# Five joined edits in a two-layer trunk: convolution taps, the end of the last FFN by token tiles, meta values and meta rows, and other parts and slots

## The chip, the cores and the metric
The kernel runs on one core of one Trainium2 chip. TensorE (PE) multiplies matrices into banks of PSUM, VectorE (DVE), ScalarE (ACT) and GpSimd (POOL) do the arithmetic on tiles in SBUF, and SyncE (SP) starts most of the transfers. The metric is the device time of one execution in microseconds (us), the median of three runs.

## The reference, cut to what matters
512 tokens of width 1024 get 16 learned "meta" rows in front, an input LayerNorm, and two layers of three residual steps each. All values are float32.

```
h = layer_norm(concat(meta, x))
for l in range(2):
    h = LN(ALPHA*h + 0.5*swiglu_ffn(h, w13_1, w2_1))      # d_ff 2752
    z = h @ w_in                                          # -> xp, ca, cg, q, k, v, g
    y_pool = trailing means of xp over 2, 4, 8, 16 tokens, minus xp, then a small matmul
    y_conv = silu(LN(causal depthwise conv, 31 taps, of ca*sigmoid(cg))) @ w_pw
    y_ret  = silu(g) * groupnorm(chunk-causal retention of q, k, v; 4 heads of 128, rotary q and k)
    h = LN(ALPHA*h + concat(y_pool, y_conv, y_ret) @ w_out)
    h = LN(ALPHA*h + 0.5*swiglu_ffn(h, w13_2, w2_2))
return h[16:]
```

## The kernel before, in words
Tokens are kept feature-major, [128 features, tokens], in eight feature tiles and two halves of 264 tokens (256 real ones and 8 meta rows each). A float32 product is made of three matmuls on split operands: high part by high part, and the two mixed ones with the rest (lines 133 to 135). So every weight tile is loaded by SP, copied rounded to its high part on ACT (L91), and its rest is taken on DVE, or on POOL for three units at the start (L94).

`enter` and `turn` bring the tokens in: the input LayerNorm runs row by row, then TensorE transposes (L257) and ACT, DVE and POOL make the split tiles (L259 to L268). Each FFN goes through its 21 full units of 128 hidden columns and a short one (21) in five `PARTS`: it makes the hidden tiles of a part, then adds that part's share to all eight output tiles (`y`), and the last part is followed by the LayerNorm of each half (`center`, `norm_apply`), whose result the next stage reads. Stages are named by layer: f0a, m0 (the mixer), f0b, f1a, m1, f1b.

The mixer makes the projections u (for the convolution) and xp (for the pools), then the values v in five token tiles (`m0v`, lines 680 to 682; the fifth is the 16 meta rows, gathered in `xm`), then per head the projections of k and q with a rotary turn (`rotary`, L703 to L705), the gate, the scores (`m0sc`, L719), and the values weighted with them. The short tile `km` holds the 16 meta columns of a head's rotated k; POOL copies them (L794), and the first score matmul of a head reads it. The convolution is 62 instructions on DVE (31 taps for two channel tiles; the first pair is a TENSOR_SCALAR on L608, the rest are on L610), issued a few at a time in the loop over the heads by `PACE`. POOL makes the sums over the pools' windows (`m0sm`, L639 and L642). `last_ffn` of layer 1 is token-major, so that its output leaves as rows; at its end come `measure`, `root`, `scale` and `leave` for each of four tiles of 128 tokens.

The program is recorded in the order of the code, and a list scheduler then sets a fixed order for each engine from its own estimates of time. Each engine works through its list in that order and waits at any instruction whose inputs, or whose buffer, are not ready. Buffers come from pools with a fixed number of slots for each tag. Those that matter here: PSUM's `acc` has four banks, used in turn by the v tiles and by the projections of k and q; `wide` has 16 slots, which hold u, xp, the convolution's sums `m0y`, and the pools' window sums.

Of the kernel before, what the change touches and what calls it, by code (L numbers as in the profile page):

```python
# [16 lines left out]
P = 128  # L17
# [23 lines left out]
PACE = (4, 3, 3, 2, 0)  # L41
# [14 lines left out]
PARTS = ([0, 1, 21, 2, 3], *(list(range(u, u + 4)) for u in (4, 8, 12)), list(range(16, 21)))  # L56


def trunk(ctx, tc, a):
# [165 lines left out]
    def enter(s):  # L225
# [47 lines left out]
    def center(tiles, n, width, name):  # L273
# [292 lines left out]
    def mixer(l, name):  # L566
# [131 lines left out]

        def rotary(ps, s, n, nm):
# [5 lines left out]
            nc.vector.tensor_tensor(out=r[:, :n], in0=r[:, :n], in1=r2[:, :n], op=ALU.add)  # L705
# [59 lines left out]
        def gate(hd, s, gg, w):  # L765
            (ps,) = project([w], s, no[s], f"{name}gp{hd}{s}")
            g = t(f"{name}gs{hd}{s}", "g")
            nc.scalar.activation(g[:, : no[s]], ps[:, : no[s]], AF.Silu)
# [77 lines left out]
    def last_ffn(l, name):  # L846
# [18 lines left out]
        for part, units in enumerate(PARTS):  # L865
# [5 lines left out]
            nk = len(full)  # L871
            for ch in range(2):
# [24 lines left out]
                if part == len(PARTS) - 1 and ch == 1:  # L897

                    for tt in range(3):
                        for i in steps:  # L900
                            step(i, tt)
                        for j in range(2):
                            add(tt, j, ps[tt][:, j * 256 : (j + 1) * 256])
                    for j in range(2):
                        o = ps[3] if j == 0 else acc(f"{name}o{ch}4")
                        for i in steps:
                            step(i, 3, j * 256, 256, o[:, :256])
                        add(3, j, o[:, :256])
                else:
                    for i in steps:  # L910
                        for tt in range(4):
                            step(i, tt)
                    for tt in range(4):
                        for j in range(2):
                            add(tt, j, ps[tt][:, j * 256 : (j + 1) * 256])
# [18 lines left out]
        def scale(tt):  # L934
            for j, y in enumerate(yt[tt]):
                if tt == 1:
# [3 lines left out]
        def leave(tt):  # L940
            g_, b_ = gb
            if tt == 1:
                nb = sq_pool.tile([P, 3], F32, tag="nb", name=f"{name}nb", bufs=2)[:, :1]
                nc.vector.scalar_tensor_tensor(out=nb, in0=mvs[tt][:, 0:1], scalar=-1.0, in1=rss[tt], op0=ALU.mult, op1=ALU.mult)
            for j in range(4):
                y = yt[tt][j][:, :256]
                if tt == 1:
                    nc.scalar.activation(y, y, AF.Identity, scale=rss[tt], bias=nb)  # L948
                    nc.gpsimd.tensor_tensor(out=y, in0=y, in1=g_[j][:, :256], op=ALU.mult)  # L949
                    nc.gpsimd.tensor_tensor(out=y, in0=y, in1=b_[j][:, :256], op=ALU.add)  # L950
                elif (tt, j) in ((2, 1), (2, 3), (3, 3)):
# [122 lines left out]
```

## Time and profile before

| | us |
|---|---|
| median of three runs | 1964.85 (1963.27 to 1964.92) |
| the profiled execution, its own time | 1963.63 |
| its span, first to last instruction | 1961.8 |
| PE busy in the span | 1907.0 (97%) |
| DVE, ACT, POOL busy | 1526.4, 909.2, 217.4 |

TensorE's granted clock has a mean of 0.994 over the span. PE is idle for 1961.8 - 1907.0 = 54.8 us. A timeline row is: start in us, duration in us, engine, line, operation, output <- inputs, shapes, count; in brackets stands how long the engine had been idle before, and what ended that.

### The profile page before, as it was taken

Reading aid. Unit: us, or ns where it says so; the run is one execution under the profiler, and the core shown is the slowest. Engines: PE = TensorE matmul, PEld = TensorE weight load, DVE = VectorE, ACT = ScalarE, POOL = GpSimd, SP = SyncE. Lnnn points to the kernel's source line nnn. Section 1 sums busy time; section 2 is a strip of 40 time slices with the busy share of each in tenths; the row PEclk is TensorE's granted clock in tenths of the full one; section 3 lists DMA queues with packets and bytes.
Section 4 is the critical chain, followed back from the end, with each engine's and each line's share of the span. In section 5 each row is a group of like instructions: output and inputs, shape, how many; then the busy total and the mean of one; then the engine's idle time right before and its main releaser. Section 6 shows DMA issues by size and latency. Waiting matters only on the chain.

```text
span 1961.8 us, 36780 instructions
## 1 busy us (share of the span) xinstructions
PE 1907.0 (97%) x14471; PEld 1824.0 (93%) x14471; DVE 1526.4 (78%) x3426; ACT 909.2 (46%) x1817; POOL 217.4 (11%) x283
## 2 busy tenths in 40 slices
PE   7999999999999999999999999999999999999996
PEld 6999999897899999999999999998889999999995
DVE  7788778689767887778696788787897686877787
ACT  5454446444333644455464454454343265544461
POOL 4000000442003000000120000005320130000001
PEclk9999999999999999999999999999999999999998
DMA  4422323322112223223223323332231213323321
GB/s 144 130 89 95 119 87 105 101 76 86 63 33 76 65 97 119 87 97 105 90 71 103 108 81 103 98 129 65 65 105 55 65 44 119 119 76 108 108 97 43
DMA packets 61068, 177.98 MB, mean 91 GB/s; under 512 B 6976, under 2 KB 10944, under 8 KB 60896
## 3 DMA queue, kind: packets, MB, share of 16 engines
q1 hardware_dynamic: 59744, 174.59, 27.9%
q8 instruction: 113, 1.85, 0.4%
q10 hardware_dynamic: 1152, 1.05, 0.2%
q14 instruction: 59, 0.48, 0.1%
HBM read 173.52 MB, written 2.10 MB: 90 GB/s over the span
## 4 chain that ended last, share of the span: by engine, by line
PE 82%; DVE 11%; issue 2%; ACT 2%; POOL 2%; DMA 0%; SPq 0%; DVEq 0%; POOLq 0%; ACTq 0%
PE f1bo L890 2%; PE f1bo L888 2%; PE f1bo L889 2%; PE f1a_y L134 2%; PE f0a_y L134 2%; PE f0b_y L134 2%; PE f1a_y L135 2%; PE f0b_y L133 2%; PE f0b_y L135 2%; PE f1a_y L133 2%; PE f0a_y L133 2%; PE f0a_y L135 2%; DVE m1y L610 1%; PE m1sc L719 1%; PE m0o L738 1%
## 5 line engine op out<-in xcount | busy, mean ns | idle before, releaser
L610 DVE SCALAR_TENSOR_TENSOR m1y<-m1u,vec,m1y 128x528 f32<-128x528 f32 x60 | 46.1, 803 | 0.0
L91 ACT CAST f0b_o_h<-f0b_o_r 128x512 fp32r<-128x512 f32 (+1 forms) x37 | 23.4, 636 | 48.7 <-PE f0b_y L134 29.6
L91 ACT CAST f0a_o_h<-f0a_o_r 128x512 fp32r<-128x512 f32 (+1 forms) x37 | 23.4, 635 | 48.6 <-PE f0a_y L134 29.5
L610 DVE SCALAR_TENSOR_TENSOR m0y<-m0u,vec,m0y 128x528 f32<-128x528 f32 x60 | 45.9, 801 | 0.0
L91 ACT CAST f1a_o_h<-f1a_o_r 128x512 fp32r<-128x512 f32 (+1 forms) x37 | 23.4, 636 | 48.4 <-PE f1a_y L134 29.6
L335 DVE TENSOR_TENSOR x<-x,f0a_y 128x264 f32<-128x264 f32 x64 | 27.2, 426 | 23.2 <-PE f0a_y L135 23.1
L335 DVE TENSOR_TENSOR h<-h,f1a_y 128x264 f32<-128x264 f32 x64 | 27.1, 425 | 23.1 <-PE f1a_y L135 23.0
L335 DVE TENSOR_TENSOR h<-h,f0b_y 128x264 f32<-128x264 f32 x64 | 27.1, 425 | 23.0 <-PE f0b_y L135 22.9
L94 DVE TENSOR_TENSOR f1bw_l<-f1bw_r,f1bw_h 128x512 fp32r<-128x512 f32 x42 | 27.7, 688 | 17.6 <-ACT f1bw_h L91 17.0
L949 POOL TENSOR_TENSOR yt<-yt,g_last 128x256 f32<-128x256 f32 x4 | 3.0, 739 | 333.2 <-ACT yt L948 333.2
L94 DVE TENSOR_TENSOR f0a_o_l<-f0a_o_r,f0a_o_h 128x512 fp32r<-128x512 f32 (+1 forms) x42 | 26.7, 642 | 13.8 <-ACT f0a_o_h L91 11.7
L94 DVE TENSOR_TENSOR f0b_o_l<-f0b_o_r,f0b_o_h 128x512 fp32r<-128x512 f32 (+1 forms) x42 | 26.6, 642 | 13.8 <-ACT f0b_o_h L91 11.7
L94 DVE TENSOR_TENSOR f1a_o_l<-f1a_o_r,f1a_o_h 128x512 fp32r<-128x512 f32 (+1 forms) x42 | 26.7, 642 | 13.7 <-ACT f1a_o_h L91 11.4
L278 POOL TENSOR_TENSOR f0b_ln_s<-h,h 128x264 f32<-128x264 f32 x2 | 1.6, 820 | 310.0 <-DVE h L335 310.0
L587 POOL MEMSET m0u<- 128x30 f32 x2 | 0.2, 123 | 304.0 <-PE f0a_20Q L135 304.0
L587 POOL MEMSET m1u<- 128x30 f32 x2 | 0.2, 123 | 303.1 <-PE f1a_20Q L135 303.1
L894 DVE TENSOR_TENSOR yt<-yt,f1bo 128x256 f32<-128x256 f32 x80 | 27.8, 415 | 5.4 <-PE f1bo L890 5.3
L91 ACT CAST f1bw_h<-f1bw_r 128x1024 fp32r<-128x1024 f32 (+1 forms) x22 | 22.1, 1011 | 21.1 <-PE f1bo L890 4.2
L291 ACT ACTIVATE m_ln_q<-h 128x264 f32<-128x264 f32 (+1 forms) x32 | 11.9, 414 | 39.7 <-DVE h L289 36.2
L257 PE MATMUL tr<-ident,xtok 128*128 128x128 f32 (+1 forms) x48 | 10.9, 328 | 11.9 <-DVE xtok L242 11.3
L257 PEld LDWEIGHTS tr<-ident,xtok 128*128 128x128 f32 (+1 forms) x48 | 6.8, 167 | 16.0 <-issue 14.7
L281 POOL TENSOR_TENSOR m_ln_s<-m_ln_s,h 128x264 f32<-128x264 f32 (+1 forms) x20 | 18.3, 914 | 30.8 <-DVE h L329 24.8
(10715 smaller groups left out, 9301.2 us busy)
## 6 DMA issues: line engine op xcount, KB each, us to landing
f1bw_r<-in_w2last SPq DMA_DIRECT2D x20, 512.0 KB, 3.9
f0a_o_r<-in_w SPq DMA_DIRECT2D x32, 256.0 KB, 2.7
f0b_o_r<-in_w SPq DMA_DIRECT2D x32, 256.0 KB, 2.8
f1a_o_r<-in_w SPq DMA_DIRECT2D x32, 256.0 KB, 2.8
m0wo_r<-in_w_out SPq DMA_DIRECT2D x8, 512.0 KB, 3.5
m1wo_r<-in_w_out SPq DMA_DIRECT2D x8, 512.0 KB, 3.5
m0w_r<-in_w_in SPq DMA_DIRECT2D x6, 512.0 KB, 4.0
m1w_r<-in_w_in SPq DMA_DIRECT2D x6, 512.0 KB, 4.2
```

The lines of the kernel that those rows point to most:

```text
L91: nc.scalar.copy(out=hi[:, :n], in_=w[:, :n])
L94: e.tensor_tensor(out=lo[:, sl], in0=w[:, sl], in1=raw(hi[:, sl]), op=ALU.subtract)
L133: nc.tensor.matmul(out, lhsT=wh, rhs=xh, start=start, stop=False, skip_group_check=onto)
L134: nc.tensor.matmul(out, lhsT=wh, rhs=xl, start=False, stop=False, skip_group_check=onto)
L135: nc.tensor.matmul(out, lhsT=wl, rhs=xh, start=False, stop=stop, skip_group_check=onto)
L335: nc.vector.tensor_tensor(out=y, in0=y, in1=ps, op=ALU.add)
L610: nc.vector.scalar_tensor_tensor(out=ys[c], in0=src, scalar=wk, in1=ys[c], op0=ALU.mult, op1=ALU.add)
L719: nc.tensor.matmul(sc[:kn, :cw], lhsT=kk[ks][:, kc : kc + kn], rhs=qq[s][:, c0 : c0 + cw], start=True, stop=True)
L888: nc.tensor.matmul(o, lhsT=hh, rhs=wh, start=part > 0 and i == 0, stop=False)
L889: nc.tensor.matmul(o, lhsT=hh, rhs=wl, start=False, stop=False)
L890: nc.tensor.matmul(o, lhsT=hl, rhs=wh, start=False, stop=i == nk - 1)
L894: nc.vector.tensor_tensor(out=y[:, :256], in0=y[:, :256], in1=o, op=ALU.add)
```

## The change
There are five edits beside each other.

1. Taps. `EARLY` = 28 of the 62 are now issued before the loop over the heads; `PACE` goes from (4, 3, 3, 2, 0) to (1, 1, 2, 2, 0), comes behind the attention's step, and each tap issued there stands behind the last rotary sum or gate.
2. The last part of `last_ffn` goes by token tiles: for one tile both halves of the output are made, then it is measured, scaled and sent. Its weights are held for the purpose, half of them in wide slots. Tiles 0 to 2 are normalised on ACT, multiplied by g on POOL (0, 1) or DVE (2), and b is added on DVE.
3. The values of the meta rows: the high and low parts stand side by side in one tile of 48 columns, so that the fifth v tile takes 16 matmuls instead of 24. Its two parts are summed into a new tile `vm`, in a wide slot, by an ACT copy and a DVE addition. POOL clears the 16 columns between.
4. `enter`: the two meta rows are normalised on ACT instead of POOL, and first.
5. `PARTS`: the second part has five units and the last four (before, the last had five). From the third of the last part's eight output tiles on, the weights are in wide slots (before: the last three). Every second tile of squares in `center` takes a slot of the tag "sm".

The diff, cut to its core:

```diff
-PACE = (4, 3, 3, 2, 0)
+EARLY, PACE = 28, (1, 1, 2, 2, 0)
-PARTS = ([0, 1, 21, 2, 3], *(list(range(u, u + 4)) for u in (4, 8, 12)), list(range(16, 21)))
+PARTS = ([0, 1, 21, 2, 3], list(range(4, 9)), *(list(range(u, u + 4)) for u in (9, 13, 17)))
...
-            for i, tt in enumerate(group):
+            for i, tt in reversed(list(enumerate(group))):
...
-                elif i == 2:
-                    nc.gpsimd.tensor_scalar(out=y, in0=y, scalar1=mv[:p, i, 0:1], scalar2=rs[:p, i : i + 1], op0=ALU.subtract, op1=ALU.mult)
...
-            q.append(t(f"{name}_q{i}", "q"))
+            q.append(t(f"{name}_q{i}", "sm" if k > 2 and i % 2 else "q"))
...
-                    make = weights_wide if part == len(PARTS) - 1 and m >= KT - 3 else weights
+                    make = weights_wide if part == len(PARTS) - 1 and m >= 2 else weights
...
-            pair = sq_pool.tile([P, 2, NM], F32R, tag="xm", name=f"{name}xm{k}", bufs=KT)
+            pair = sq_pool.tile([P, 48], F32R, tag="xm", name=f"{name}xm{k}", bufs=KT)
+            nc.gpsimd.memset(raw(pair[:, NM:32]), 0.0)
...
+                if tt == 4:
+
+                    nc.tensor.matmul(ps[:48], lhsT=xm[k], rhs=wh, start=k == 0, stop=False)
+                    nc.tensor.matmul(ps[:48], lhsT=xm[k], rhs=wl, start=False, stop=k == KT - 1)
+                    continue
...
+            if tt == 4:
+                vm = wide(f"{name}vm")
+                nc.scalar.copy(out=vm[:n, :512], in_=ps[32 : 32 + n])
+                nc.vector.tensor_tensor(out=vm[:n, :512], in0=ps[:n], in1=vm[:n, :512], op=ALU.add)
+                ps = vm[:, :512]
...
+            made["last"] = nc.vector.tensor_tensor(out=r[:, :n], in0=r[:, :n], in1=r2[:, :n], op=ALU.add).ins
...
         taps = conv_taps()
+        for _ in range(EARLY):
+            next(taps)
...
-                for _ in range(PACE[hd]):
-                    next(taps, None)
                 if hd == HEADS or i > 0:
                     next(steps, None)
+                with tc.issue_after(made["last"]):
+                    for _ in range(PACE[hd]):
+                        next(taps, None)
...
+        for tt in range(4):
+            ts = slice((tt % 2) * P, (tt % 2 + 1) * P)
+            for ch in range(2):
+                for c, cw in ((0, 256), (256, 256)) if (tt, ch) == (3, 1) else ((0, 512),):
...
             measure(tt)
             root(tt)
-            if tt == 3:
-                with tc.issue_after(met[tt]):
-                    leave(2)
             scale(tt)
-            if tt != 2:
-                leave(tt)
+            leave(tt)
```

What this does to the engines' lists is shown at three places. The first is DVE in the mixer of layer 0, from the fourth v tile's column sum (m0vmu from m0v) to the first head's k times its cosine (m0k00r). Rows of m0y are taps; a row ending in m0w..._l is the rest of a weight split. Before:

```order
L684 TENSOR_REDUCE m0vmu_5671<-m0v_5646 128x4
L610 SCALAR_TENSOR_TENSOR m0y_5474<-m0u_5114,vec,m0y_5474 128x528
L685 TENSOR_SCALAR m0vmu_5671<-m0vmu_5671 128x4
L610 SCALAR_TENSOR_TENSOR m0y_5475<-m0u_5184,vec,m0y_5475 128x528
L94 TENSOR_TENSOR m0wq_l<-m0wq_r,m0wq_h 128x512 x2
...
L94 TENSOR_TENSOR m0wk_l<-m0wk_r,m0wk_h 128x512 x2
L684 TENSOR_REDUCE m0vmu_5705<-m0v_5680 16x4
...
L610 SCALAR_TENSOR_TENSOR m0y_5475<-m0u_5184,vec,m0y_5475 128x528
L703 TENSOR_TENSOR m0k00r<-m0kp_0_5738,cosb 128x264
```

Now, from the same column sum on:

```order
L693 TENSOR_REDUCE m0vmu_5670<-m0v_5645 128x4
L694 TENSOR_SCALAR m0vmu_5670<-m0vmu_5670 128x4
L94 TENSOR_TENSOR m0wq_l<-m0wq_r,m0wq_h 128x512 x2
L94 TENSOR_TENSOR m0wk_l<-m0wk_r,m0wk_h 128x512 x2
L606 TENSOR_SCALAR m0y_5465<-m0u_5105,vec 128x528
L690 TENSOR_TENSOR m0vm<-m0v_5679,m0vm 16x512
L606 TENSOR_SCALAR m0y_5466<-m0u_5175,vec 128x528
L693 TENSOR_REDUCE m0vmu_5699<-m0vm 16x4
L608 SCALAR_TENSOR_TENSOR m0y_5465<-m0u_5105,vec,m0y_5465 128x528
...
L643 TENSOR_TENSOR m0sm_2_5745<-m0sm_2_5745,inv_n 128x16
L645 SCALAR_TENSOR_TENSOR m0xp_5238<-m0sm_2_5745,inv_n,m0xp_5238 128x512
L714 TENSOR_TENSOR m0k00r<-m0kp_0_5760,cosb 128x264
```

Before, taps lie between the column sums of all v tiles. Now no tap lies ahead of the fourth one's sum, the first stands beside `vm`, which needs the fifth v tile, and all 28 early taps stand in one run (the dots: 25 more of them and the other row of the fifth column sum) ahead of m0k00r. The lists of layer 1's mixer read the same.

The second place is POOL in the same mixer, behind the last gathered meta columns of the layer. Before:

```order
L670 CAST m0xm_5511<-f0a_ln_x7l 128x8
L642 TENSOR_TENSOR m0sm_1_5720<-m0xp_5247 128x542
L639 COPY m0sm_2_5723<-m0sm_1_5720 128x2
L642 TENSOR_TENSOR m0sm_2_5723<-m0sm_1_5720 64x541
L639 COPY m0sm_1_5891<-m0xp_5418 128x1
```

Now:

```order
L669 CAST m0xm_5509<-f0a_ln_x7l 128x8
L666 MEMSET m1xm_17742 128x16
...
L666 MEMSET m1xm_17784 128x16
L637 COPY m0sm_1_5742<-m0xp_5238 128x1
L640 TENSOR_TENSOR m0sm_1_5742<-m0xp_5238 128x542
L637 COPY m0sm_2_5745<-m0sm_1_5742 128x2
```

Eight clears of the next layer's `xm` now stand ahead of the window sums. They reuse the slots that the fifth v tile's matmuls read, so they wait for those.

The third place is POOL at the start of the program, from the meta rows' normalisation (xtok) to the rest of the eighth token tile (x_7_0_l). Before:

```order
L244 TENSOR_SCALAR xtok_97<-xtok_97,in_mv,in_y 8x512
L244 TENSOR_SCALAR xtok_98<-xtok_98,in_mv,in_y 8x512
L94 TENSOR_TENSOR f0a_0u_l<-f0a_0u_r,f0a_0u_h 128x512 x2
L268 TENSOR_TENSOR x_1_0_l<-x_1_0_165,x_1_0_h 128x264
L268 TENSOR_TENSOR x_3_0_l<-x_3_0_185,x_3_0_h 128x264
L268 TENSOR_TENSOR x_5_0_l<-x_5_0_205,x_5_0_h 128x264
L268 TENSOR_TENSOR x_7_0_l<-x_7_0_225,x_7_0_h 128x264
```

Now:

```order
L266 TENSOR_TENSOR x_1_0_l<-x_1_0_165,x_1_0_h 128x264
L94 TENSOR_TENSOR f0a_0u_l<-f0a_0u_r,f0a_0u_h 128x512
L266 TENSOR_TENSOR x_3_0_l<-x_3_0_185,x_3_0_h 128x264
L94 TENSOR_TENSOR f0a_0u_l<-f0a_0u_r,f0a_0u_h 128x512
L94 TENSOR_TENSOR f0a_1u_l<-f0a_1u_r,f0a_1u_h 128x512
L266 TENSOR_TENSOR x_5_0_l<-x_5_0_205,x_5_0_h 128x264
L94 TENSOR_TENSOR f0a_1u_l<-f0a_1u_r,f0a_1u_h 128x512
L94 TENSOR_TENSOR f0a_21w_l<-f0a_21w_r,f0a_21w_h 128x512 x2
L266 TENSOR_TENSOR x_7_0_l<-x_7_0_225,x_7_0_h 128x264
```

The two meta rows have left POOL, and the splits of two more weight tiles (f0a_1u and f0a_21w) have moved ahead of x_7_0_l.

## Rows read from the trace of the kernel before

**Rows 1.** The page, busy time of each engine.

```profile
PE 1907.0 (97%) x14471; PEld 1824.0 (93%) x14471; DVE 1526.4 (78%) x3426; ACT 909.2 (46%) x1817; POOL 217.4 (11%) x283
```

**Rows 2.** Stretches: bounds, length, each engine's busy us (instructions), granted clock, DMA share, GB/s.

```profile
0.00:20.00 20.00, 8.05 (x30) 5.39 (x31) 14.24 (x40) 8.50 (x15) 8.57 (x13) 1.00 0.74 256
380.00:400.00 20.00, 17.88 (x131) 16.24 (x130) 17.66 (x51) 11.02 (x23) 13.52 (x27) 1.00 0.33 104
440.00:460.00 20.00, 20.00 (x120) 15.52 (x119) 20.00 (x37) 8.38 (x21) 0.00 (x0) 1.00 0.12 39
460.00:480.00 20.00, 16.29 (x111) 14.72 (x111) 20.00 (x41) 9.22 (x17) 12.29 (x4) 0.91 0.48 141
1940.00:1962.00 22.00, 4.27 (x33) 3.92 (x32) 18.36 (x64) 3.60 (x7) 8.49 (x11) 0.69 0.28 96
```

**Rows 3.** Timeline of PE, mixer of layer 0, fifth v tile to first scores.

```profile
446.29 0.40 PE L680 MATMUL m0v<-m0wv_h,m0xm 128*16 128x512 f32 x1
...
451.82 0.28 PE L133 MATMUL m0kp<-f0a_ln_x0h,m0wk_h 128*128 128x264 f32 x1
...
463.48 0.28 PE L133 MATMUL m0kp<-f0a_ln_x0h,m0wk_h 128*128 128x264 f32 x1
...
472.85 0.62 PE L719 MATMUL m0sc<-m0q00r,m0km 128*16 128x264 f32 x2 [3.38 <-POOL m0km L794]
```

**Rows 4.** Timeline of DVE in the same mixer.

```profile
424.21 4.31 DVE L610 SCALAR_TENSOR_TENSOR m0y<-m0u,vec,m0y 128x528 f32<-128x528 f32 x5
...
430.55 5.38 DVE L610 SCALAR_TENSOR_TENSOR m0y<-m0u,vec,m0y 128x528 f32<-128x528 f32 x5
...
442.78 4.15 DVE L610 SCALAR_TENSOR_TENSOR m0y<-m0u,vec,m0y 128x528 f32<-128x528 f32 x6
446.86 0.68 DVE L684 TENSOR_REDUCE m0vmu<-m0v 128x4 f32<-128x512 f32 x1
...
454.31 1.28 DVE L94 TENSOR_TENSOR m0wq_l<-m0wq_r,m0wq_h 128x512 fp32r<-128x512 f32 x2
...
461.15 0.41 DVE L703 TENSOR_TENSOR m0k00r<-m0kp,cosb 128x264 f32<-128x264 f32 x1
...
466.11 0.41 DVE L705 TENSOR_TENSOR m0k01r<-m0k01r,m0k01r 128x264 f32<-128x264 f32 x1
```

**Rows 5.** Timeline of POOL in the same mixer.

```profile
432.26 1.74 POOL L642 TENSOR_TENSOR m0sm<-m0sm 64x535 f32<-64x535 f32 x1
463.06 3.76 POOL L794 COPY m0km<-m0k00r 128x8 f32<-128x8 f32 x1 [29.06 <-DVE m0k00r L705]
466.77 6.03 POOL L794 COPY m0km<-m0k01r 128x8 f32<-128x8 f32 x1
474.26 1.35 POOL L794 COPY m0km<-m0k10r 128x8 f32<-128x8 f32 x1 [1.46 <-DVE m0k10r L705]
```

**Rows 6.** Timelines of DVE and PE, the same place in layer 1.

```profile
1431.00 0.41 DVE L703 TENSOR_TENSOR m1k00r<-m1kp,cosb 128x264 f32<-128x264 f32 x1
1442.65 0.60 PE L719 MATMUL m1sc<-m1q00r,m1km 128*16 128x256 f32 x2 [3.54 <-POOL m1km L794]
```

**Rows 7.** Timeline of POOL at the start.

```profile
10.64 4.45 POOL L244 TENSOR_SCALAR xtok<-xtok,in_mv,in_y 8x512 f32<-8x512 f32 x2 [9.31 <-DVE in_y L177]
...
22.35 0.75 POOL L268 TENSOR_TENSOR x_l<-x,x_h 128x264 fp32r<-128x264 f32 x1 [0.54 <-ACT x_h L266]
23.29 2.98 POOL L94 TENSOR_TENSOR f0a_1u_l<-f0a_1u_r,f0a_1u_h 128x512 fp32r<-128x512 f32 x2 [0.20 <-ACT f0a_1u_h L91]
```

**Rows 8.** Timeline of DVE from the first FFN into the mixer.

```profile
366.98 2.81 DVE L289 TENSOR_TENSOR x<-x,f0a_ln_mean 128x264 f32<-128x264 f32 x8 [0.81 <-PE f0a_ln_mean L283]
...
384.21 1.29 DVE L308 SCALAR_TENSOR_TENSOR x<-x,vec,f0a_ln_rs 128x264 f32<-128x264 f32 x3
```

**Rows 9.** Timeline of DVE at the end.

```profile
1944.31 0.42 DVE L894 TENSOR_TENSOR yt<-yt,f1bo 128x256 f32<-128x256 f32 x1
...
1956.79 1.74 DVE L955 SCALAR_TENSOR_TENSOR yt<-yt,f1brs_y,b_last 128x256 f32<-128x256 f32 x3
```

More of the change, by code (lines that the diff above doesn't have):

```diff
@@ L666, in mixer @@
         for k in range(KT):
-            pair = sq_pool.tile([P, 2, NM], F32R, tag="xm", name=f"{name}xm{k}", bufs=KT)
+            pair = sq_pool.tile([P, 48], F32R, tag="xm", name=f"{name}xm{k}", bufs=KT)
+            nc.gpsimd.memset(raw(pair[:, NM:32]), 0.0)
             for p_ in range(2):
                 for s in range(2):
-                    nc.gpsimd.tensor_copy(pair[:, p_, s * HM : (s + 1) * HM], raw(xs[k][s][p_][:, 256:NT]))
-            xm.append((pair[:, 0, :], pair[:, 1, :]))
+                    nc.gpsimd.tensor_copy(pair[:, 32 * p_ + s * HM : 32 * p_ + (s + 1) * HM], raw(xs[k][s][p_][:, 256:NT]))
+            xm.append(pair)
         vt = {}
@@ L697, in mixer @@
             nc.sync.dma_start(out=wpw[k][:, :256], in_=a["pw"][l][:, k * 256 : (k + 1) * 256])
+        made = {}
         def rotary(ps, s, n, nm):
@@ L704, in rotary @@
             nc.vector.tensor_tensor(out=r2[:, :n], in0=r2[:, :n], in1=sinb[:, s, :n], op=ALU.mult)
-            nc.vector.tensor_tensor(out=r[:, :n], in0=r[:, :n], in1=r2[:, :n], op=ALU.add)
+            made["last"] = nc.vector.tensor_tensor(out=r[:, :n], in0=r[:, :n], in1=r2[:, :n], op=ALU.add).ins
             return r
@@ L767, in gate @@
             g = t(f"{name}gs{hd}{s}", "g")
-            nc.scalar.activation(g[:, : no[s]], ps[:, : no[s]], AF.Silu)
+            made["last"] = nc.scalar.activation(g[:, : no[s]], ps[:, : no[s]], AF.Silu).ins
             gg.append(g)
@@ L871, in last_ffn @@
             nk = len(full)
+            if part == len(PARTS) - 1:
+                break
             for ch in range(2):
@@ L896, in last_ffn @@
                 steps = range(-1 if part == 0 else 0, nk)
[L897 to L903, printed above, removed]
-                    for j in range(2):
[L905 to L915, printed above, removed]
+                for i in steps:
+                    for tt in range(4):
+                        step(i, tt)
+                for tt in range(4):
+                    for j in range(2):
+                        add(tt, j, ps[tt][:, j * 256 : (j + 1) * 256])
             done += nk
@@ L935, in scale @@
             for j, y in enumerate(yt[tt]):
-                if tt == 1:
+                if tt < 3:
                     break
@@ L941, in leave @@
             g_, b_ = gb
-            if tt == 1:
-                nb = sq_pool.tile([P, 3], F32, tag="nb", name=f"{name}nb", bufs=2)[:, :1]
+            if tt < 3:
+                nb = sq_pool.tile([P, 3], F32, tag="nb", name=f"{name}nb{tt}", bufs=2)[:, :1]
                 nc.vector.scalar_tensor_tensor(out=nb, in0=mvs[tt][:, 0:1], scalar=-1.0, in1=rss[tt], op0=ALU.mult, op1=ALU.mult)
@@ L946, in leave @@
                 y = yt[tt][j][:, :256]
-                if tt == 1:
+                if tt < 3:
                     nc.scalar.activation(y, y, AF.Identity, scale=rss[tt], bias=nb)
-                    nc.gpsimd.tensor_tensor(out=y, in0=y, in1=g_[j][:, :256], op=ALU.mult)
-                    nc.gpsimd.tensor_tensor(out=y, in0=y, in1=b_[j][:, :256], op=ALU.add)
-                elif (tt, j) in ((2, 1), (2, 3), (3, 3)):
+                    e = nc.gpsimd if tt < 2 else nc.vector
+                    e.tensor_tensor(out=y, in0=y, in1=g_[j][:, :256], op=ALU.mult)
+                    nc.vector.tensor_tensor(out=y, in0=y, in1=b_[j][:, :256], op=ALU.add)
+                elif j % 2:
                     nc.scalar.mul(y, y, rss[tt])
@@ L956, in leave @@
                 (nc.sync if j % 2 else nc.scalar).dma_start(out=a["out"][tt * P : (tt + 1) * P, j * 256 : (j + 1) * 256], in_=y)
-        for tt in range(4):
+        c0 = done * 512
+        w_last = [[], []]
+        for i in range(0, nk, 2):
+            cw = min(2, nk - i) * 512
+            for ch, make in enumerate((weights, weights_wide)):
+                w = make(a["w2last"][ch, :, c0 + i * 512 : c0 + i * 512 + cw], cw, f"{name}l{ch}{i}")
+                w_last[ch] += w if ch else [at(w, slice(c, c + 512)) for c in range(0, cw, 512)]
+        for tt in range(4):
+            ts = slice((tt % 2) * P, (tt % 2 + 1) * P)
+            for ch in range(2):
+                for c, cw in ((0, 256), (256, 256)) if (tt, ch) == (3, 1) else ((0, 512),):
+                    o = acc(f"{name}l{tt}{ch}{c}")
+                    for i in range(nk):
+                        wh, wl = (x[:, c : c + cw] for x in w_last[ch][i])
+                        hh, hl = at(hid[full[i]][tt // 2], ts)
+                        nc.tensor.matmul(o[:, :cw], lhsT=hh, rhs=wh, start=i == 0, stop=False)
+                        nc.tensor.matmul(o[:, :cw], lhsT=hh, rhs=wl, start=False, stop=False)
+                        nc.tensor.matmul(o[:, :cw], lhsT=hl, rhs=wh, start=False, stop=i == nk - 1)
+                    for k in range(0, cw, 256):
+                        y = yt[tt][2 * ch + (c + k) // 256]
+                        nc.vector.tensor_tensor(out=y[:, :256], in0=y[:, :256], in1=o[:, k : k + 256], op=ALU.add)
             measure(tt)
             root(tt)
-            if tt == 3:
-                with tc.issue_after(met[tt]):
-                    leave(2)
             scale(tt)
-            if tt != 2:
-                leave(tt)
+            leave(tt)
     load_tokens((4, 0, 1))
```

2 lines of the change are left out of this document (1 added, 1 removed).

## The prediction

> **What bounds the kernel now.** I read the busy time of the engines first. The reader is to see that PE is busy for 97% of the span [rows 1], so that the end moves only where PE's idle time or its number of matmuls does: 54.8 us of idle time in all. The second view is the table of stretches, to find where that idle time lies [rows 2]: 12.0 us at the start, 2.1 in the last 20 us ahead of the mixer, 3.7 in the mixer between 460 and 480, and 17.7 at the end. Between 440 and 460 PE is full, and DVE is full too, through 480. A stage with both engines full has nothing to give to a DVE list that becomes worse. The third view is the timelines of the mixer [rows 3 to 5]. The reader is to follow one chain there. PE makes the fifth v tile from 446.29, four projections of k and q from 451.82, and the next two (for the second head) from 463.48. DVE takes the first of them up at 461.15 (m0k00r) and has the sum of the second half's k at 466.11. POOL copies the meta columns (m0km) at 463.06 and 466.77, and PE, which had been idle for 3.38 us, begins the scores at 472.85. So from m0k00r to the scores it is 472.85 - 461.15 = 11.7 us, and this chain already sets PE's time before.
>
> **The change in the mixer, step by step.** The fifth v tile takes 451.82 - 446.29 = 5.53 us for 24 matmuls, 0.230 each [rows 3]. With 16 it takes 3.69, and PE is 1.84 us earlier: it begins the projections at 449.98, and after the four of them (463.48 - 451.82 = 11.66 us) it stands at 461.64 before the first one for the second head. That one goes into the first of the four accumulator banks again, and this bank is not free until DVE has made m0k00r from it. So I need the new time of m0k00r.
>
> DVE's list decides it. All 28 early taps now stand behind the sum for `vm`, and ahead of m0k00r. The sum needs the fifth v tile, at 449.98, and an ACT copy, for which no row of before stands; I take it as the 0.68 us of the column sum, which reads as many columns [rows 4]. So the sum begins at about 450.7 and ends at about 451.3; the two pairs of weight rests ahead of it (1.28 us a pair [rows 4]) lie beside the fifth v tile, from the fourth's column sum at 446.86 on. One tap can go beside the ACT copy, which leaves 27. Six taps take 4.15 us [rows 4], 0.69 each: 27 x 0.69 = 18.6, to 469.9. The column sum of `vm` adds 0.68 and its scaling some 0.15, and three instructions of the pool's mean, of a tap's kind or smaller, about 1.0: m0k00r at 471.8 at the earliest.
>
> To this comes POOL. Its window sums stand behind clears that wait for the fifth v tile, so they run beside the taps. Five taps took 4.31 and another five 5.38 us while POOL was on such sums [rows 4, 5], against 3.46 at 0.69 each: 0.85 and 1.92 more. The same sums beside the new run cost about 2.8 in all, which makes 474.6. I take 473.0, between the two, since the last sums may begin only when early taps are past: 11.85 us later than before.
>
> A rule of the Trainium skill speaks to this ("SBUF — State Buffer", section "Who interferes with whom"): a DVE instruction with two SBUF inputs and a POOL instruction that reads SBUF exclude each other, and the later one blocks until the first ends. The rows agree that they disturb each other, but ten taps lost only 2.8 us beside sums such as the 1.74 us one; with full exclusion the whole of POOL's time would be added. That result is the third rival below.
>
> From m0k00r on, the chain to the scores is as before: the list has the sum of the first half's k two places later, and then the second's. POOL's two copies took 3.76 and 6.03 us [rows 5], both beside a DVE that is full, and it will be full again. 473.0 + 11.7 = 484.7 against 472.85: 11.85 us later. The two projections that PE makes in the meantime are not what ends last: from 473.4 they take half of 11.66 us, 5.8, or twice that at half the clock, to 485.0 at most. PE will be idle from 461.6 to about 473.4. The 1.84 us saved are swallowed by this wait. I take +12 for each mixer; in layer 1 the same distance stands, 1442.65 - 1431.00 = 11.65 [rows 6], and the same list: +24 for both.
>
> The price from both sides. Low: the third km copy took only 1.35 us [rows 5]. Were the first ones as short, it would be 471.8 + (466.11 + 0.41 - 461.15 = 5.4) + 1.35 = 478.5: +5.7. High: with the sums' 2.8 us and 2 more for the casts, m0k00r at 476.5, and +15.4. The nearest row is that of the copies themselves, so I stay near 12.
>
> Nothing gives it back: before, PE was full in this stage, and the taps not yet done at the scores are more than before (28 and a few are done of 62, where before some 43 were). These 10 to 15 taps of 0.69 us go into the heads, whose DVE time they lengthen by 7 to 10 us. Between 0 and 4 us for each mixer can come of that, at the convolution's norm; I take +1: +2 for both.
>
> **The other parts.** *Start.* The meta rows on POOL took 4.45 us, and they leave it [rows 7]; but f0a_1u (2.98 us) and f0a_21w, of the same size, now stand ahead of x_7_0_l, which before ended at 23.1. POOL therefore gives 4.45 and takes 5.96, and its x rows also wait for ACT, which has taken the meta rows and makes the high parts of the same weights. PE idles for what x_7_0_l is late. Bounds: -1.5 (only the earlier transposes count) to +6 (the two splits in full). I take +2.5, nearer the difference of 1.5 plus ACT's share.
>
> *Ends of the three feature-major FFNs.* From the centring at 366.98 to the applied norm at 384.21 it is 17.2 us [rows 8], and in it lie eight rests of weights for the mixer (0.64 each, by the pair of 1.28 in [rows 4]). Half of them have moved ahead, which shortens the chain by 2.6 us, and more slots for squares and weights loosen it. Against it, the last part has four units instead of five, so the matmuls that cover the chain are fewer: eight output tiles of 3 matmuls at 11.66 / 96 = 0.121 [rows 3], 2.9 us. As PE is idle for just 2.1 us there [rows 2], no end can give much more than that. I take -1 for each of the three, and -0.5 for each norm behind a mixer: -4, between -8 and +3.
>
> *The last end.* The last DVE work ends at 1956.79 + 1.74 = 1958.5, 14.2 us after the last sum with PE's result began at 1944.31 [rows 9]. By token tiles the tiles 0 to 2 are nearly through by then, and what is left is one tile's chain: two statistics, the root's small steps, four scalings and four additions. I count 12 to 14 us: -1.5, between -3 and 0.
>
> **The sum.** The profiled execution took 1963.63 us, within the runs shown (1963.27 to 1964.92) and 1.2 below their median; I add no correction. 1963.6 + 24 + 2 + 2.5 - 4 - 1.5 = 1986.6, forecast 1987. The change is slower by 1.1%.
>
> **The rivals.** *Short wait.* The km copies are short, because the new list has fewer taps beside them: one per step. Then each mixer costs 5.7, and the sum is 1963.6 + 11.4 + 1 + 2.5 - 5.5 = 1973. For it speaks the third copy's 1.35 us; against it, that DVE's rotary work reads SBUF as the taps do and is as dense.
>
> *No wait: the other side.* The early taps run in the idle time that DVE has beside the v tiles, so that m0k00r comes no later than PE's 461.64. Then nothing is lost, the 1.84 us of matmuls are gained twice, with up to the 3.38 of idle time ahead of the scores: 1963.6 - 3.7 - 3.4 + 2.5 - 5.5 = 1953.5, and about 1957 without the latter. It decides from the point at which m0k00r comes before 463 instead of after 471. Nothing in the lists lets a tap start ahead of the fourth column sum, so it would need that the run is not the one printed; or parts 2 and 5 would have to give over 25 us, more than the idle time in their stretches.
>
> *Full exclusion.* Each tap waits for POOL's whole instruction. POOL's sums are some eight of 1.7 us or less, about 8 to 12 us, in place of the 1 to 3 counted: m0k00r at about 480, +19 for each mixer, and 1963.6 + 38 + 2 + 2.5 - 5.5 = 2000.6.
>
> *The wait goes elsewhere.* If the start costs its 6 and the ends give nothing, the forecast's case stands at 1996; this is its upper part.
>
> **Chances.** The forecast's case (1980 to 1996) 0.63; short wait (1966 to 1980) 0.18; full exclusion (above 1996) 0.11; no wait, or gains that outweigh it (below 1966) 0.08. The range reaches from the middle of the short wait to the middle of full exclusion: 1970 to 1999. A measurement of this kernel can tell 0.2%, about 4 us, from no change; below 1961 I put 0.05, between 1961 and 1969 0.04, above 0.91.
>
> **What would show it.** In the profile after: PE idle for about 12 us in each mixer, between the fourth and the fifth projection of k and q, waiting for DVE's m0k00r; that instruction some 20 us after the fifth v tile and behind an unbroken run of 28 taps; DVE idle between the column sums of the v tiles; the scores 11 to 12 us after m0k00r; a granted clock below 1 in that stretch. The start's loss would show as idle PE ahead of f0a_0's last matmuls, and the boundaries as less idle time ahead of the mixers. The forecast is wrong if m0k00r comes within 5 us of the fifth v tile's last matmul plus the four projections, or if PE has other work during that run.

## The result, and the profile after

The changed kernel takes 1995.86 us in the median of four runs (1992.77 to 1997.17), the kernel before 1964.61. The ratio is 1.0158, with a 95% interval of 1.0141 to 1.0176: 31 us slower, where 1987 had been forecast and a range of 1970 to 1999. The profiled execution is the fastest of the four: 1992.77 us, with a span of 1991.0.

The page of the changed kernel, busy time of each engine, answers to [rows 1]:

```profile
PE 1911.7 (96%) x14452; PEld 1828.0 (92%) x14452; DVE 1530.3 (77%) x3431; ACT 914.2 (46%) x1823; POOL 201.1 (10%) x294
```

PE has 19 matmuls fewer in the record and 4.7 us more of busy time, and 79.3 us of idle time instead of 54.8. The stretches of the changed kernel, columns as in [rows 2], with the mixer of layer 0 between 440 and 500:

```profile
0.00:20.00 20.00, 8.67 (x32) 5.98 (x33) 13.62 (x41) 9.65 (x16) 1.87 (x17) 1.00 0.71 246
20.00:40.00 20.00, 16.75 (x119) 15.38 (x117) 14.73 (x31) 10.61 (x19) 10.94 (x9) 1.00 0.31 106
380.00:400.00 20.00, 17.35 (x120) 15.82 (x119) 17.27 (x47) 6.61 (x18) 14.20 (x24) 0.91 0.17 54
440.00:460.00 20.00, 20.00 (x104) 15.88 (x103) 7.98 (x14) 9.08 (x20) 4.72 (x12) 1.00 0.16 47
460.00:480.00 20.00, 7.46 (x62) 7.25 (x60) 19.01 (x31) 1.28 (x4) 19.94 (x3) 0.75 0.08 27
480.00:500.00 20.00, 15.99 (x80) 14.01 (x80) 15.20 (x34) 7.22 (x15) 6.78 (x11) 0.74 0.00 1
1969.00:1991.00 22.00, 5.84 (x37) 5.05 (x36) 16.98 (x70) 5.17 (x10) 4.63 (x6) 0.72 0.22 74
```

Read the third number of a row (PE) beside the fifth (DVE). Between 440 and 460 PE is full and DVE busy for 7.98 us; then DVE is full and PE busy for 7.46. Before, both were full in the first of these stretches. POOL's 19.94 us in only three instructions are the surprise of the table.

The timeline of PE in that mixer, from the fifth v tile to the first scores, answers to [rows 3]:

```profile
451.90 0.39 PE L680 MATMUL m0v<-m0wv_h,m0xm 128*48 128x512 f32 x1
...
481.01 0.59 PE L133 MATMUL m0kp<-f0a_ln_x0h,m0wk_h 128*128 128x264 f32 x1 [13.55 <-DVE m0k00r L714]
...
490.17 0.60 PE L730 MATMUL m0sc<-m0q00r,m0km 128*16 128x264 f32 x2 [0.39 <-DVE m0q00r L716]
```

The first matmul of the second head stands for 13.55 us and waits for m0k00r, as forecast. DVE in the same place, which answers to [rows 4]:

```profile
452.17 0.69 DVE L693 TENSOR_REDUCE m0vmu<-m0v 128x4 f32<-128x512 f32 x1 [4.68 <-PE m0v L686]
...
457.11 1.32 DVE L606 TENSOR_SCALAR m0y<-m0u,vec 128x528 f32<-128x528 f32 x1
458.36 0.67 DVE L690 TENSOR_TENSOR m0vm<-m0v,m0vm 16x512 f32<-16x512 f32 x1
...
460.76 17.05 DVE L608 SCALAR_TENSOR_TENSOR m0y<-m0u,vec,m0y 128x528 f32<-128x528 f32 x25
...
480.54 0.42 DVE L714 TENSOR_TENSOR m0k00r<-m0kp,cosb 128x264 f32<-128x264 f32 x1
...
484.74 0.43 DVE L714 TENSOR_TENSOR m0k01r<-m0kp,cosb 128x264 f32<-128x264 f32 x1 [2.57 <-ACT m0k01r L713]
```

DVE idles 4.68 us ahead of the column sum, and likewise ahead of the two before it; then come the first tap, vm, the run of taps in one row, and m0k00r 22.2 us after vm. In the kernel before, the first tap begins ahead of the first v tile:

```profile
421.38 0.54 DVE L608 TENSOR_SCALAR m0y<-m0u,vec 128x528 f32<-128x528 f32 x1
```

POOL in the changed kernel, which answers to [rows 5]:

```profile
456.60 1.55 POOL L640 TENSOR_TENSOR m0sm<-m0xp 128x542 f32<-128x542 f32 x1
...
458.56 20.20 POOL L640 TENSOR_TENSOR m0sm<-m0sm 64x541 f32<-64x541 f32 x1
...
478.99 1.60 POOL L640 TENSOR_TENSOR m0sm<-m0xp 128x542 f32<-128x542 f32 x1
...
485.64 0.60 POOL L805 COPY m0km<-m0k00r 128x8 f32<-128x8 f32 x1 [0.71 <-DVE m0k00r L716]
```

One window sum takes 20.20 us, from just ahead of the taps' run to just behind it; the sums next to it, of the same line, take 1.55 and 1.60 us. The table of waits (who waited for whom: total us, times, longest) shows what stood behind it, and the two waits of PE with the one at the start:

```profile
ACT m0sm L639 <- POOL m0sm L640: 21.1, 1, 21.1
...
PE m0kp L133 <- DVE m0k00r L714: 13.6, 1, 13.6
...
PE m1kp L133 <- DVE m1k00r L714: 11.0, 1, 11.0
...
PE f0a_0p L134 <- POOL x_l L266: 2.9, 2, 2.2
```

In layer 1 the same run of taps stands in the same place, but its window sums were done more than 20 us earlier. DVE and PE there, which answer to [rows 6]:

```profile
1446.71 17.05 DVE L608 SCALAR_TENSOR_TENSOR m1y<-m1u,vec,m1y 128x528 f32<-128x528 f32 x25
...
1464.53 0.41 DVE L714 TENSOR_TENSOR m1k00r<-m1kp,cosb 128x264 f32<-128x264 f32 x1
1473.26 0.60 PE L730 MATMUL m1sc<-m1q00r,m1km 128*16 128x256 f32 x2
```

POOL at the start, which answers to [rows 7]: x_l of the eighth token tile ends at 31.0 instead of 23.1, behind f0a_21w's two rests.

```profile
27.55 2.75 POOL L94 TENSOR_TENSOR f0a_21w_l<-f0a_21w_r,f0a_21w_h 128x512 fp32r<-128x512 f32 x2
30.27 0.73 POOL L266 TENSOR_TENSOR x_l<-x,x_h 128x264 fp32r<-128x264 f32 x1
```

And the end, PE's last matmul and DVE's last work, which answers to [rows 9]:

```profile
1974.56 0.28 PE L980 MATMUL f1bl<-f1bl_h,f1b_20x_l 128*128 128x256 f32 x1
1985.98 0.88 DVE L959 SCALAR_TENSOR_TENSOR yt<-yt,f1brs_y,b_last 128x256 f32<-128x256 f32 x2
```

Where the 29.2 us of span come from is read from the first matmul of each stage, by tile, in both traces:

| stretch, from first matmul to first matmul | before | after | difference |
|---|---|---|---|
| start to m0pu (of it by f0a_2p: 54.2, 58.2) | 385.3 | 389.7 | +4.4 (+4.0) |
| m0pu to m0kp: u, xp, v | 66.5 | 65.9 | -0.6 |
| m0kp to m0sc | 21.0 | 34.5 | +13.5 |
| m0sc to f0b_0p: heads, output, norm | 153.2 | 158.1 | +4.9 |
| f0b_0p to m1pu: two FFNs | 728.1 | 728.1 | 0.0 |
| m1pu to m1kp | 67.4 | 66.0 | -1.4 |
| m1kp to m1sc | 21.1 | 30.9 | +9.8 |
| m1sc to f1b_0p | 147.5 | 147.7 | +0.2 |
| f1b_0p to the end | 371.6 | 370.0 | -1.6 |

### The profile page after: what moved, and what is told of

Read it like the earlier page. It is cut to its first block, busy times and chain, and to the rows that moved or that the text cites. A ratio compares the mean times of both kernels' runs of the same rounds, so it can differ in the third digit from the quotient of the medians.

```text
span 1991.0 us, 36735 instructions
## 1 busy us (share of the span) xinstructions
PE 1911.7 (96%) x14452; PEld 1828.0 (92%) x14452; DVE 1530.3 (77%) x3431; ACT 914.2 (46%) x1823; POOL 201.1 (10%) x294
## 4 chain that ended last, share of the span: by engine, by line
PE 65%; issue 16%; DVE 11%; ACT 2%; POOL 2%; DMA 1%; POOLq 0%; ACTq 0%; DVEq 0%
PE f1a_y L134 2%; PE f0b_y L134 2%; PE f0a_y L134 2%; PE f1a_y L135 2%; PE f0a_y L135 2%; PE f0b_y L135 2%; PE f1a_y L133 2%; PE f0b_y L133 2%; PE f0a_y L133 2%; POOL m0sm L640 1%; DVE m1y L608 1%; DVE h L287 1%; PE m0o L749 1%; PE m1o L749 1%; PE m0sc L730 1%
## 5 line engine op out<-in xcount | busy, mean ns | idle before, releaser
L94 DVE TENSOR_TENSOR f0b_o_l<-f0b_o_r,f0b_o_h 128x512 fp32r<-128x512 f32 (+1 forms) x42 | 25.2, 614 | 12.3 <-ACT f0b_o_h L91 10.7
L94 DVE TENSOR_TENSOR f1bw_l<-f1bw_r,f1bw_h 128x512 fp32r<-128x512 f32 x34 | 22.4, 689 | 14.0 <-ACT f1bw_h L91 13.6
L910 DVE TENSOR_TENSOR yt<-yt,f1bo 128x256 f32<-128x256 f32 x64 | 22.1, 416 | 8.1 <-PE f1bo L906 8.1
L91 ACT CAST f1bw_h<-f1bw_r 128x1024 fp32r<-128x1024 f32 (+1 forms) x18 | 17.9, 1003 | 17.3 <-PE f1bo L906 4.2
L640 POOL TENSOR_TENSOR m0sm<-m0sm 64x541 f32<-64x541 f32 (+3 forms) x4 | 23.7, 5927 | 0.2
```

The costliest lines, as they stand in the source:

```text
L91: nc.scalar.copy(out=hi[:, :n], in_=w[:, :n])
L94: e.tensor_tensor(out=lo[:, sl], in0=w[:, sl], in1=raw(hi[:, sl]), op=ALU.subtract)
L640: nc.gpsimd.tensor_tensor(out=dst[b:, w_:], in0=cur[b:, w_:], in1=cur[b:, : W - w_], op=ALU.add)
L910: nc.vector.tensor_tensor(out=y[:, :256], in0=y[:, :256], in1=o, op=ALU.add)
```

## The experiments

Two theories were set against each other. A: the place of the taps is what costs; the convolution's sums get their wide slots behind `vm`, so no tap starts ahead of the fifth v tile. B: the number of early taps is what costs, wherever they begin. All ratios are to the kernel before, in runs on the same chip.

**First pair of taps ahead of vm.** The edit to the changed kernel:

```diff
+        taps = conv_taps()
+        for _ in range(2):
+            next(taps)
         xm = []
...
-        taps = conv_taps()
-        for _ in range(EARLY):
+        for _ in range(EARLY - 2):
             next(taps)
```

> The changed kernel, with one edit: the first pair of the 28 early taps is issued ahead of the code that makes xm and vm, the other 26 stay where they were; the number of taps, the meta values with vm and all other parts are those of the change. In the list of DVE the taps now lie beside the v tiles again, and vm stands alone between the weight rests and m0k00r. Theory A (slot order: the convolution's sums get their wide slots behind vm, so no tap can start before the fifth v tile): the loss in both mixers, about 25 of the 31 us, goes, and the 1.84 us of matmuls for each mixer are gained: 1963 to 1968 us, PE's wait for m0k00r below 2 us. Theory B (28 taps issued as one block ahead of the heads are too many for DVE, wherever they begin): the wait stays above 8 us in each mixer, 1985 us or more.

Measured: 1966.85 us, ratio 1.0008 (0.9999 to 1.0018). 29 us are back from moving two instructions in the text, with all 28 early taps, vm and everything else kept. B fails. In the table of waits of this run, PE's wait for m0k00r is gone, and one of 5.1 us is left in layer 0, which has no partner in layer 1:

```profile
PE m0sc L734 <- DVE m0sm L745: 5.1, 1, 5.1
```

There the window sums still stand behind the clears of xm. The expectation spoke only of the wait for m0k00r and did not foresee this loss, which is larger than the one wait: from m0sc to f0b_0p it takes 163.3 us, before 153.2.

**Meta values as before, taps as changed.** `xm`, the 24 matmuls and the missing `vm` are taken from the kernel before.

> The changed kernel with the meta values as before (24 matmuls, no vm, no clears), and with the 28 early taps and the new PACE kept. Theory A: without vm in a wide slot the taps can start beside the v tiles; 1963 to 1969 us, no wait of PE for m0k00r above 2 us in either mixer, and DVE busy over 18 of 20 us beside the v tiles. Theory B: the block of 28 still delays m0k00r; above 1985 us.

Measured: 1962.92 us, ratio 0.9992 (0.9983 to 1.0002). The block of 28 alone does no harm. Its stretch from 440 to 460 (columns as in [rows 2]) has PE and DVE filled beside each other, though DVE a little less than the 18 us expected:

```profile
440.00:460.00 20.00, 20.00 (x93) 14.19 (x93) 17.54 (x33) 8.50 (x20) 0.78 (x1) 1.00 0.15 39
```

These two runs show that the taps start early again (at 415.3 and 419.7 us) when their first pair is issued ahead of vm, or when there is no vm. That it is the slot is inferred from the code, where vm and the convolution's sums take slots of the same tag; it fits that the first tap of the changed kernel begins at 457.11, just behind ACT's first write into vm at 456.84. A vm in a tag of its own was not tried.

**Taps as before, meta values as changed.**

```diff
-EARLY, PACE = 28, (1, 1, 2, 2, 0)
+EARLY, PACE = 0, (4, 3, 3, 2, 0)
...
+                for _ in range(PACE[hd]):
+                    next(taps, None)
                 if hd == HEADS or i > 0:
                     next(steps, None)
-                with tc.issue_after(made["last"]):
-                    for _ in range(PACE[hd]):
-                        next(taps, None)
```

> The changed kernel with the taps as before (none early, 4, 3, 3, 2 for each step, ahead of the attention's step), and vm kept. Theory B: without the block of 28 the wait for m0k00r goes and the time falls to 1964 to 1970 us. Theory A: the taps still begin only behind vm, so DVE stays idle for some 20 us beside the v tiles; m0k00r comes early (within 5 us of vm), but then four taps stand between the steps, and PE loses the time in several shorter waits at the projections and scores: 1978 to 1990 us.

Measured: 1991.14 us, ratio 1.0133 (1.0116 to 1.0151), just above A's range and far from B's. Without any early tap nearly the whole loss stays. It only moves: m0k00r now comes early, and PE waits behind taps at the scores instead. Its table of waits:

```profile
PE m0sc L730 <- DVE m0sm L741: 12.7, 3, 10.1
PE m1sc L730 <- DVE m1sm L741: 12.4, 3, 8.4
```

**Both as before.** What is left of the change is parts 2, 4 and 5.

> The changed kernel with both the taps and the meta values as before; what is left of the change is the meta rows on ACT at the start, the other parts and slots, and the last FFN by token tiles. The trace of the changed kernel puts the start at +4.0 us (first matmul of f0a_2p at 58.2 instead of 54.2), the stretches between the mixers at about +0.4 and what follows the last mixer at -1.6. If these are independent of the mixers, this run takes 1965 to 1969 us. A rival (theory C: the parts and slots also cost time inside the mixers): above 1972 us.

Measured: 1967.62 us, ratio 1.0015 (1.0005 to 1.0026). Parts 2, 4 and 5 add about 3 us in sum. C fails.

**The start alone.** Only the meta rows on ACT, on the kernel before.

> The kernel before with only the meta rows of the start on ACT and first (part 4). The list of POOL then has two weight tiles' rests ahead of the rest of the eighth token tile, as in the changed kernel. Theory A (the parts are independent; the trace of the changed kernel shows +4.0 us by the first matmul of f0a_2p): 1967 to 1970 us, PE waiting 2 to 3 us for POOL's x_l ahead of f0a_0's last matmuls. Rival (the start's loss in the changed kernel comes from the eight clears of xm that now stand on POOL at the start): within 1 us of the kernel before.

Measured: 1971.48 us, ratio 1.0039 (1.0024 to 1.0054), 1.5 us above its range. In its trace f0a_2p begins at 57.9 instead of 54.2, and the whole span is 3.7 longer, with the wait of the changed kernel and without a clear on POOL, so the rival fails:

```profile
PE f0a_0p L134 <- POOL x_l L266: 2.9, 2, 2.2
```

Its runs lie between 1967.3 and 1976.3, and the median is 4 us above the profiled run. Why this kernel's runs spread so far stays open.

**Parts and slots alone.** Only part 5 on the kernel before.

> The kernel before with only part 5: parts of 5, 5, 4, 4, 4 units, wide slots for the weights of six output tiles, and squares in two tags. Theory A: the rest's chain ahead of a mixer gets shorter, the cover too; -1 us for each of three ends, 1960 to 1965 us, with the first matmul of m0pu 0 to 2 us earlier than before. Rival (the smaller cover outweighs it): 1966 to 1970 us.

Measured: 1967.10 us, ratio 1.0013 (1.0004 to 1.0022): the rival's side. In its trace m0pu begins at 385.4 (before 385.3) and f1a_0p at 989.4 (989.5): nothing is gained ahead of these stages. m1pu is 1.4 later, and from f1b_0p to the end it takes 374.3 instead of 371.6.

**The end by token tiles alone.** Only part 2, with five units in the last part.

> The kernel before with only the end of the last FFN by token tiles (part 2), its last part still of five units. Theory A: -1.6 us, as the stretch from the last FFN's first matmul to the end was shorter in the changed kernel: 1961 to 1964 us. Rival: that gain belongs to the shorter last part (four units), and the token tiles alone give nothing or lose: 1964 to 1968 us.

Measured: 1960.93 us, ratio 0.9982 (0.9974 to 0.9991). From f1b_0p to the end it takes 368.9 instead of 371.6. The gain belongs to the token tiles, and it is larger than the 1.6 us seen in the joined kernel. There part 5 takes from it: alone, it makes this stretch 2.7 us longer, as the run with parts and slots alone showed.

**A mended join.** The changed kernel with the first pair of taps and all window sums ahead of xm and vm, and the start as before.

```diff
+        pool_y = {c: pool_windows(c) for c in range(2)}
         xm = []
...
-            if hd < 2:
-                pool_y[hd] = pool_windows(hd)
```

> The changed kernel with three things mended: the first pair of early taps and all pool window sums are issued ahead of xm and vm, and the start is as before (meta rows on POOL). Theory A: the first run of this study took 1966.9 us; from it go the 5.1 us wait in layer 0's mixer (the window sums no longer stand behind the clears) and about 4 us at the start: 1956 to 1960 us, the fastest of all. Rival (POOL's sums beside the dense taps cost as much as they give): 1962 us or more.

Measured: 1953.61 us, ratio 0.9948 (0.9936 to 0.9960), 2.4 us under its range. From m0sc to f0b_0p it takes 153.8 us, 9.5 less than in the run with only the taps ahead, so the late window sums had cost more than the 5.1 us counted for them. No wait of PE is left between the projections and the scores of layer 0; the stretch from 460 to 480, beside [rows 2]:

```profile
460.00:480.00 20.00, 20.00 (x145) 17.77 (x143) 15.64 (x36) 7.38 (x13) 2.61 (x3) 1.00 0.33 103
```

**Window sums early, taps late.** The changed kernel with only the window sums moved ahead of xm.

> The changed kernel, with the pool window sums issued ahead of xm and vm, so that they no longer stand behind the clears in layer 0; the 28 taps still stand in one run behind vm. In the changed kernel one window sum of layer 0 took 20.2 us beside that run (1.1 to 1.6 us elsewhere), ACT stood behind it for 21.1 us, and PE waited 13.6 us for m0k00r against 11.0 in layer 1, where the sums were done before. Theory A' (the run of taps starves POOL, and ACT with it; that is the difference between the layers): layer 0 becomes like layer 1, PE waits 10 to 11.5 us in each, and the time falls by 2 to 5 us against the changed kernel, to 1991 to 1994 us. Rival (POOL slows the taps, the rule read the other way): the run of 25 taps, 17.05 us beside POOL, becomes clearly shorter, by 2 us or more.

Measured: 1985.12 us, ratio 1.0107 (1.0093 to 1.0121): 10.7 us less than the changed kernel, where 2 to 5 were expected. The run of taps takes the same time to the digit with an idle POOL, and the two layers wait alike:

```profile
461.46 17.05 DVE L608 SCALAR_TENSOR_TENSOR m0y<-m0u,vec,m0y 128x528 f32<-128x528 f32 x25
```

```profile
PE m1kp L133 <- DVE m1k00r L715: 10.1, 1, 10.1
PE m0kp L133 <- DVE m0k00r L715: 10.0, 1, 10.0
```

So in the changed kernel the window sums did not slow the taps; the taps held up one window sum, and ACT behind it. This is not how the two share everywhere. In the mended join, sums and an equally dense row of taps take turns:

```profile
424.67 9.78 DVE L610 SCALAR_TENSOR_TENSOR m0y<-m0u,vec,m0y 128x528 f32<-128x528 f32 x9
...
427.63 1.63 POOL L642 TENSOR_TENSOR m0sm<-m0sm 128x541 f32<-128x541 f32 x1
...
429.83 1.61 POOL L642 TENSOR_TENSOR m0sm<-m0sm 128x539 f32<-128x539 f32 x1
```

Nine taps take 9.78 us there, 1.09 each instead of 0.68, and no sum lasts longer than 1.74 us beside them; the kernel before does the same in [rows 4, 5]. What decides between the two, no run here shows. In the run with early window sums, from m0kp to m0sc it is 29.3 us instead of 34.5, and from m0sc to f0b_0p 153.6 instead of 158.1: the 4.9 us that layer 0 lost after the scores, and layer 1 did not, were the same stall, carried on into the heads.

**The mended join with the parts as before**, and then **with the squares in two tags put back**.

> The best version so far (1953.6 us) with part 5 undone as well: PARTS, wide weights and squares as before. Theory A (part 5 alone cost +1.3 per thousand, about 2.6 us, and is independent of the rest): 1949 to 1952 us. Rival (part 5's four-unit last part is needed by the token tiles' end, which keeps all of its weights at once): 1954 us or more.

> The kernel before with only the squares in two tags, from part 5. If part 5's loss of 2.6 us lies in the parts of 5, 5, 4, 4, 4 units, this run is within 1 us of the kernel before or up to 3 us faster; if it lies in the slots shared with the squares, it is 2 us or more slower.

> The version with parts as before (1954.0 us), with the squares in two tags put back. Alone on the kernel before they gave 2.5 us (0.9988). Theory A (that gain lies in the norms ahead of the next stage and is independent): 1950 to 1953 us. Rival (the gain was shared with the parts that are already in): 1953 to 1955 us.

Measured: the first 1953.97 us, ratio 0.9951 (0.9937 to 0.9965), above its range and no better than with part 5, so the independence assumed there does not hold. Its rival's reason does not hold either: from f1b_0p to the end it takes 368.6 us with the old parts and 369.4 in the mended join, so the token tiles do not need the last part of four units. The squares alone on the kernel before: 1961.85 us, ratio 0.9988 (0.9979 to 0.9996); in the trace m0pu begins 1.3 us earlier and m1pu 2.4. The mended join with the squares and with the old parts: 1950.41 us, ratio 0.9930 (0.9917 to 0.9944), the fastest of all, 0.7% under the kernel before. Its page:

```profile
PE 1902.5 (98%) x14455; PEld 1821.8 (94%) x14455; DVE 1535.4 (79%) x3431; ACT 911.7 (47%) x1828; POOL 200.5 (10%) x298
```

So within part 5 the squares gain, and the new parts with the wide weights lose about what the squares gain or more. Which of the two it is was not tried.

## Why the prediction was right, point by point

*The mixer's wait* was right in its mechanism and nearly in its size. Forecast were PE's idle time between the fourth and fifth projection (about 12 us; 13.6 and 11.0 measured), an unbroken run of taps, an idle DVE between the v tiles, and a granted clock below 1 (0.75 and 0.74 in two stretches of layer 0). The sum for both mixers was +26 with the taps left over; the table's six rows of the mixers give -0.6 + 13.5 + 4.9 - 1.4 + 9.8 + 0.2 = 26.4. The experiments show the cause: with two taps moved ahead of vm, PE's wait for m0k00r goes. By layers the same rows are 17.8 and 8.6, where I had put 13 on each.

*Its inner steps* were less good than that sum. I had m0k00r 23.0 us after the fifth v tile's end and then the full 11.7 us to the scores, as POOL's copies of 3.76 and 6.03 us [rows 5] should last. Measured from the fifth v tile's end at 455.6, m0k00r came after 24.9 us in layer 0; in layer 1 the corresponding distance is 1464.5 - 1442.4 = 22.1. But the copies took 0.60 and 0.67 us. DVE's list now has single taps there, and idle time such as the 2.57 us ahead of m0k01r, which I take to be the reason; it was not tried apart. From m0k00r to the scores it was 9.6 and 8.7 us. The rival of the short wait had this part right, without its conclusion: what then ended last, but for 0.39 us, was PE's own two projections. After 13.55 us of idle time PE ran them at the lower of its two levels for a while (1.2 instead of 2.4 GHz): matmuls came every 0.22 us, not 0.12, and the first 24 took 5.45 us. The granted clock, the third number from the end, is 0.50 there:

```profile
481.00:486.50 5.50, 5.49 (x25) 5.49 (x26) 2.93 (x5) 3.16 (x5) 4.32 (x6) 0.50 0.00 0
```

I had named the length of two projections at half the clock and thought it covered.

*POOL beside the taps.* I counted 1 to 3 us for taps slowed by window sums, from [rows 4, 5], and gave the full exclusion, by which each would add to the other, a chance of 0.11. For this run of taps the direction was wrong: it took 0.68 us a tap whether POOL worked or not, and POOL finished one sum in 20 us. My reading of [rows 4, 5] was also too mild. Beside the ten taps' 2.8 us, the two weight rests between them lost 0.9 (2.17 us instead of 1.28), and the four sums 1.9 against the run with early window sums (1.54 to 1.74 each instead of 1.08 to 1.34), which is not far from each waiting for the other's whole instruction; and the sums are six in a layer, not some eight. In layer 0 the held-up sum cost about 5 us up to the scores and 5 more behind them, by the run with early window sums, so the two layers were not alike as I had assumed. That the sum still came out is a coincidence in part: the copies were cheaper than forecast, and the stall dearer.

*The start* was +4.0 instead of +2.5, inside its bounds: POOL's rests ahead of x_7_0_l and PE's wait of 2.9 us for it were as forecast, and the run with the start alone shows it apart from the clears.

*The ends of the FFNs* are the term that failed: -4 forecast (1 of it for the norms behind the mixers, which lie in the mixers' rows), +0.4 for the first end and 0.0 for both FFNs between the mixers. The chain did shorten, by more than the 2.6 us counted: from the centring to the applied norm it is 388.62 - 375.28 = 13.3 us, where it was 17.2 in [rows 8]. Nine rests of weights lay in it, not eight, and five have moved ahead.

```profile
375.28 2.81 DVE L287 TENSOR_TENSOR x<-x,f0a_ln_mean 128x264 f32<-128x264 f32 x8 [0.80 <-PE f0a_ln_mean L281]
...
388.62 1.29 DVE L306 SCALAR_TENSOR_TENSOR x<-x,vec,f0a_ln_rs 128x264 f32<-128x264 f32 x3
```

But the centring begins at 375.28 instead of 366.98, and the later start accounts for only 4.0 of these 8.3 us. With part 5 alone, where the start is as before, the chain is 13.4 us and begins 4.0 later. What I had set against the gain, 2.9 us of cover, thus came out at about 4 and took all of it back; whether the four units or the wide weights do that was not tried apart. The squares alone give about 1 us an end.

Something I had at nothing stands just behind this end: the granted clock falls to its lower level at the mixer's start, which it does not before ([rows 2] have 1.00 from 380 to 400).

```profile
392.00:394.00 2.00, 2.00 (x10) 1.93 (x9) 0.83 (x3) 0.92 (x2) 1.43 (x7) 0.50 0.00 0
```

From the first matmul of m0pu to that of m0v it takes 39.9 us, before 38.7. With the squares alone the clock falls there too (0.50 from 384 to 386), and only 0.4 of the 1.3 us gained are left at m0v. PE's waits just ahead of m0pu, 0.68 and 0.89 us, are the same in that run and in the kernel before, so why the clock falls in the one and not in the other stays open.

The term of the ends is most of the distance between 1987 and the profiled 1992.8; the start's 1.5 is the rest of it. The median lies another 3.1 above that execution, a spread of the changed kernel's runs that I had not allowed for.

*The tail* was -1.5 forecast, -1.6 measured; from PE's last matmul to DVE's last work it is 12.0 us instead of 14.3.

## What to carry to other kernels

Before joining edits that were each tried alone, read the order of each engine's list for what stands ahead of what: here one small new tile, taken between two others from what is by the code a shared pool, held back 62 instructions that do not touch it, and issuing two of them earlier in the text undid 29 us. A busy share does not show this: DVE was busy for 1530.3 us against 1526.4 before, but its first tap began at 457.1 instead of 421.4. And a POOL instruction beside a dense run of VectorE work should be priced from both sides: it lasted as long as the run in the changed kernel, and took turns with the taps in the mended join.

## What the runs showed of the hardware

A dense run of VectorE instructions that read two SBUF tiles held up one POOL addition for 20.20 us (1.09 us in the run with early window sums) and was itself not slowed: 25 taps in 17.05 us with POOL waiting and with POOL idle. The Trainium skill ("SBUF — State Buffer", section "Who interferes with whom") says that the later of two such instructions blocks until the first ends. The trace agrees that POOL blocks; but it waited for the whole run of 25, not for the one instruction that had come first. In the mended join an equally dense row of nine taps let the sums through one by one and took 1.09 us a tap, so the one outcome is not the rule.

TensorE began at the lower level (granted clock 0.50 from 481.0 to 486.5) after 13.55 us without work, and two dozen matmuls took 5.45 us, where the same ones took 2.9 in the kernel before [rows 3].
